# Moving the projections' shared elementwise work from GpSimd to the vector engine

## The chip, the cores and the metric

The kernel runs on one core of one Trainium2 chip. The metric is the device time of one execution in microseconds (us). The engines are named as the profile names them: PE is TensorE's matmul side and PEld its weight loads, DVE is the vector engine (VectorE), ACT is ScalarE, POOL is GpSimd, SP is SyncE, which only issues transfers here. Each engine carries out its own queue of instructions in order.

## The reference, cut to what matters

A trunk of two layers works on x of 1024 tokens by 1024 channels, float32:

```python
for l in range(2):
    h = rmsnorm(x, norm1_w[l])
    q, k, v, g, z, xbc, dt, gate, xin = split_proj(h @ w_in[l])
    y = concat([retention(q, k, v, g),            # 256 wide
                ssd(z, xbc, dt, ...),             # 512 wide
                rglru(gate, xin, ...)], -1)       # 256 wide
    x = x + y @ w_out[l]
    h = rmsnorm(x, norm2_w[l])
    u, v = split(causal_dwconv(h @ w_up[l]))      # 2 x 2816 wide, width-3 conv
    x = x + (gelu(u) * v) @ w_down[l]
return rmsnorm(x, final_norm_w)
```

The three mixers (retention, SSD, RG-LRU) are causal; what matters here is the four projections of each layer (into the mixers, out of them, up and down of the gated MLP).

## The kernel before, in words

**Layout.** Channels lie on the 128 partitions and tokens on the free axis, in two halves of 512 tokens. Almost every tile is 128 x 512 float32.

**Split operands.** A projection is computed at near float32 accuracy from operands split in two: ACT copies a tile to the matmul's type (the high part), and an elementwise subtraction `raw - high` gives the low part; three matmuls (high x high, high x low, low x high, the tuple `PASSES`) then stand for one. Weights arrive raw by DMA and are split on the chip in `part_split` (called by `part_of` and `wsplit`), activations in `split` and `load_split`. The subtraction of a weight's split has two forms. In the ordinary form it is one tensor-tensor instruction on DVE or on POOL. In the other, ACT first writes `-high` and POOL issues a DMA that adds the raw tile to it (`pool.dma_start(..., accum_op=ALU.add)`, "the accumulating transfer"). The flag `by_dma` allows the second form, and it is up only in the steady part of `products`.

**Who makes the low part.** `lo_engine` counts its calls and gives one call in `share` to DVE and the others to POOL; `share` is 3, and 2 inside `ffn_down`:

```python
    flip, share = [0], [3]

    def lo_engine():
        flip[0] += 1
        return dve if flip[0] % share[0] == 0 else pool
```

**Seven products for eight.** The up and in projections (`products`, class `Pair`) and the down projection (`ffn_down`) multiply 2 x 2 blocks in Strassen-Winograd form, so there are extra additions and subtractions of blocks, of weights (`Pair.prep`) and of activations (`blocks_b`); `sub(engine, ...)` (L714) carries out each one.

**Stages of a layer.**

- In projection: `blocks_a` or `blocks_raw` and `blocks_b` scale the activations by the norm, form the blocks t1, t2, t3, t4, b22 and split them, while the first pairs of outputs are already computed; then `products` goes through 12 pairs of output tiles with `by_dma` up.
- Mixers (`mixers`), with some work of POOL's own (L562, L563, L604, and L366, L370 in `lru`).
- Out projection (`out_proj`): 16 tiles of weights split by `wsplit`, mixer outputs loaded and split by `load_split` (L215, tiles `yl`), residual added (L699), and `squares` and `norm_sum` for the next norm. `squares` gives 6 of 8 squares to an accumulator on DVE and 2 to one on POOL; `norm_sum` adds both up on PE (tile `nst`).
- Up projection: `blocks_a`, `blocks_b` again, then `products` over 22 pairs, with convolution (L322) and gate (L939); results go to DRAM.
- Down projection (`ffn_down`): the *first loop*, 11 turns of 24 matmuls of 128 x 512 (tiles `dy`, `dx`, L1001) with four splits and three subtractions of activations each; then two more loops of 11 turns, and `last` (or `last` and `rest` in the second layer).

**What sets the order.** The kernel states each engine's instructions in program order, and a scheduler of the language then sets the order in each engine's queue before the program runs; it uses dependencies and its own estimates. The order on the chip is fixed.

## Time and profile before

| | |
|---|---|
| median of 3 runs | 2451.67 us (2446.18 to 2458.61) |
| the profiled execution, its own time | 2448.8 us |
| its span in the profile | 2447.0 us |
| PE matmuls busy | 2220.8 us, 91% of the span |
| DVE busy | 1967.6 us, 80% |
| ACT busy | 1278.5 us, 52% |
| POOL busy | 1096.3 us, 45% |
| mean granted TensorE clock | 0.963 of full speed |

The profile is one execution. Its page gives busy time and instruction counts by engine, the busiest groups of instructions, the waits and the transfers. A group is named by its source line, its engine, its operation and the tiles it writes and reads (`ws<-wr,ws`: the split weight tile `ws` from the raw tile `wr` and `ws` itself). An instruction's duration runs from its start to its end and includes the time in which it is held up after its start. PE's busy time is modelled and overlaps from one matmul to the next, so the pace of matmuls is read from their number in a stretch.

### The profile page before, as it was taken

The page shows a single profiled execution, that of the slowest core. Times are in us where ns is not written, and L with a number is a line of the kernel's source. Part 1 is how long each engine was busy: PE and PEld are TensorE (multiplying, and loading weights), DVE is VectorE, ACT ScalarE, POOL GpSimd, SP SyncE. Part 2 cuts the span into 40 slices and gives each one's busy share as a digit, 9 for nine tenths or more (in the row PEclk, how much of TensorE's full clock was granted, in tenths as well). Part 3 has the DMA queues.
Part 4 walks back from the last instruction along what each step waited for, and adds up shares of the span by engine and source line. Part 5 has one row for each costly group of instructions (what it writes and reads, how often), then busy time and mean ns, then how long its engine had stood idle before and what let it go on. Part 6 is the DMA issues. An engine that isn't in the chain of part 4 may idle for free. (4 is left out here: it accounts for less than half of the span.)

```text
span 2447.0 us, 32235 instructions
## 1 busy us (share of the span) xinstructions
PE 2220.8 (91%) x10646; PEld 1771.0 (72%) x10646; DVE 1967.6 (80%) x3242; ACT 1278.5 (52%) x2370; POOL 1096.3 (45%) x846
## 2 busy tenths in 40 slices
PE   5788978997999999989988988889989999998997
PEld 4566767775888888767765766777768888876776
DVE  7997768668888888887788876695797888889787
ACT  4356647454565666334444664664555665653343
POOL 4534433346434433554655332333473443437443
PEclk8999999998999999999989999999999999999999
DMA  4364685551666666843334647845426666575521
GB/s 175 103 149 115 162 255 192 163 188 44 141 158 150 146 147 159 273 156 123 104 112 125 152 108 203 260 135 184 145 71 163 148 159 157 139 231 182 168 70 70
DMA packets 176151, 371.98 MB, mean 152 GB/s; under 512 B 19440, under 2 KB 31856, under 8 KB 175984
## 3 DMA queue, kind: packets, MB, share of 16 engines
q1 hardware_dynamic: 135760, 297.55, 37.5%
q0 software_dynamic: 37440, 68.17, 16.6%
q10 hardware_dynamic: 2784, 4.20, 0.5%
q8 instruction: 84, 1.38, 0.2%
q14 instruction: 83, 0.68, 0.1%
HBM read 228.22 MB, written 69.27 MB: 122 GB/s over the span
## 5 line engine op out<-in xcount | busy, mean ns | idle before, releaser
L304 PE MATMUL up<-bh,ws 128*128 128x512 f32 x3840 | 1222.4, 399 | 59.8 <-ACT ws L235 33.4
L304 PEld LDWEIGHTS up<-bh,ws 128*128 128x128 f32 x3840 | 736.0, 192 | 229.9 <-ACT ws L235 35.2
L304 PE MATMUL up<-bl,ws 128*128 128x512 f32 x1920 | 763.8, 399 | 38.4 <-DVE bl L203 19.4
L235 ACT ACTIVATE ws<-wr 128x512 fp32r<-128x512 f32 x568 | 345.3, 621 | 304.9 <-issue 75.4
L304 PEld LDWEIGHTS up<-bl,ws 128*128 128x128 f32 x1920 | 368.2, 192 | 134.5 <-DVE bl L203 29.0
L242 POOL TENSOR_TENSOR ws<-wr,ws 128x512 fp32r<-128x512 f32 x164 | 241.8, 1483 | 268.1 <-ACT ws L235 252.2
L240 POOL DMA_DIRECT2D ws<-wr x222 | 198.4, 910 | 252.4 <-ACT ws L239 151.4
L714 POOL TENSOR_TENSOR wr<-wr 128x512 f32<-128x512 f32 x64 | 104.7, 1635 | 347.3 <-DVE wr L714 214.8
L1001 PE MATMUL dy<-ws,ws 128*128 128x512 f32 x792 | 214.0, 410 | 26.8 <-DVE ws L242 14.9
L1001 PEld LDWEIGHTS dy<-ws,ws 128*128 128x128 f32 x792 | 148.0, 194 | 83.7 <-DVE ws L242 35.0
L1001 PE MATMUL dx<-ws,ws 128*128 128x512 f32 x792 | 193.7, 393 | 4.1 <-DVE u L896 3.8
L1001 PEld LDWEIGHTS dx<-ws,ws 128*128 128x128 f32 x792 | 149.3, 189 | 37.7 <-DVE u L896 4.7
L322 DVE SCALAR_TENSOR_TENSOR fc<-c,smalls,fc 128x512 f32<-128x512 f32 (+2 forms) x176 | 175.1, 995 | 1.6 <-ACT fc L319 1.4
L242 DVE TENSOR_TENSOR ws<-wr,ws 128x512 fp32r<-128x512 f32 x182 | 142.0, 781 | 37.3 <-ACT ws L235 33.9
L322 DVE SCALAR_TENSOR_TENSOR fc<-u,smalls,fc 128x512 f32<-128x512 f32 (+2 forms) x176 | 140.4, 800 | 35.4 <-ACT fc L319 32.6
L304 PE MATMUL op<-yh,ws 128*128 128x512 f32 x512 | 165.2, 402 | 2.2 <-ACT yh L210 2.2
L239 ACT ACTIVATE ws<-ws 128x512 fp32r<-128x512 f32 x260 | 159.5, 625 | 4.6
L319 ACT ACTIVATE fc<-c,smalls 128x512 f32<-128x512 f32 x88 | 71.3, 810 | 131.2 <-DVE c L843 128.4
L242 DVE TENSOR_TENSOR ws<-g,ws 128x512 fp32r<-128x512 f32 (+1 forms) x94 | 113.0, 1229 | 29.9 <-ACT ws L235 29.7
L714 POOL TENSOR_TENSOR wr<-wr,s 128x512 f32<-128x512 f32 x64 | 103.4, 1615 | 58.3 <-DVE s L714 50.1
L714 DVE TENSOR_TENSOR wr<-wr,wr 128x512 f32<-128x512 f32 x64 | 45.1, 704 | 87.4 <-DMA wr<-in_w_up_dram 41.1
L304 PEld LDWEIGHTS op<-yh,ws 128*128 128x128 f32 x512 | 97.1, 192 | 23.0 <-ACT yh L210 3.3
(319 smaller groups left out, 3576.1 us busy)
## 6 DMA issues: line engine op xcount, KB each, us to landing
ws<-wr POOLq DMA_DIRECT2D x222, 256.0 KB, 4.2
wr<-in_w_up_dram SPq DMA_DIRECT2D x96, 512.0 KB, 4.4
wr<-in_w_dn_dram SPq DMA_DIRECT2D x66, 512.0 KB, 3.6
wr<-in_w_ct_dram SPq DMA_DIRECT2D x56, 512.0 KB, 4.3
wr<-in_w_o_dram SPq DMA_DIRECT2D x32, 512.0 KB, 4.7
g0scr<-fc SPq DMA_DIRECT2D x44, 256.0 KB, 3.6
g<-g0scr SPq DMA_DIRECT2D x44, 256.0 KB, 5.7
g1scr<-fc SPq DMA_DIRECT2D x44, 256.0 KB, 3.6
```

Source lines behind the costliest of these rows:

```text
L235: act.activation(w[:, 0, :m], raw, AF.Copy)
L239: act.activation(w[:, 1, :m], w[:, 0, :m].bitcast(F32), AF.Copy, scale=-1.0)
L240: pool.dma_start(w[:, 1, :m].bitcast(F32), raw, accum_op=ALU.add)
L242: eng.tensor_tensor(w[:, 1, :m], raw, w[:, 0, :m].bitcast(F32), op=ALU.subtract)
L304: pe.matmul(dst, W(k, a), A(k, b), start=first and i == 0, stop=last and i == n - 1)
L319: act.activation(dst, body(x), AF.Identity, bias=bias, scale=taps(n))
L322: dve.scalar_tensor_tensor(dst[:, o:HT], x[:, HALO - j + o : HALO - j + HT], taps(n - j), dst[:, o:HT], op0=ALU.mult, op1=ALU.add)
L714: eng.tensor_tensor(o, a, b, op=op)
L1001: pe.matmul(d[oc], w[:, a, P * oc : P * oc + P], t[:, b], start=not more and i == 0 and k == 0, stop=i == NP - 1 and k == 2, skip_group_ch ...
```

## The change

Elementwise work outside the mixers that POOL shared goes to DVE. `lo_engine` gives POOL only while `by_dma` is up, and whatever `part_split` gives to POOL is then the accumulating transfer. `squares` keeps one accumulator, on DVE. `blocks_b`, `Pair.scaled`, `Pair.prep` and `ffn_down` name DVE where they named POOL. POOL keeps the 260 accumulating transfers, its instructions in the mixers and a few of the final norm. The core of the diff:

```diff
-    flip, share = [0], [3]
+    flip = [0]
+
+    by_dma = [False]
     def lo_engine():
         flip[0] += 1
-        return dve if flip[0] % share[0] == 0 else pool
+        return pool if by_dma[0] and flip[0] % 3 else dve
...
     def part_split(w, raw, m, eng=None):
         act.activation(w[:, 0, :m], raw, AF.Copy)
         eng = eng or lo_engine()
-        if eng is pool and by_dma[0]:
+        if eng is pool:
...
-    def squares(X, spare=False, n=HT, f=t_tile):
-        acc = {}
-        for k in range(KD):
-            x = X(k)
-            eng = pool if k in (3, 6) else dve
...
+    def squares(X, n=HT, f=t_tile):
+        acc = f("nacc")[:, :n]
+        act.activation(acc, X(0), AF.Square)
+        for k in range(1, KD):
+            sq = f("nsq")[:, :n]
+            act.activation(sq, X(k), AF.Square)
+            dve.tensor_tensor(acc, acc, sq, op=ALU.add)
+        return [acc]
...
-            split(hi, lo, src, dve if name in ("t1", "b22") else engines[k % 2])
+            split(hi, lo, src, dve)
...
-                engines[i % 4 == 3].tensor_tensor(x, x, rows, op=ALU.mult)
+                dve.tensor_tensor(x, x, rows, op=ALU.mult)
...
-            sub(pool, XA[4 + k], XA[4 + k], t)
+            sub(dve, XA[4 + k], XA[4 + k], t)
...
-            sub(engines[k % 2], XB[k], XB[4 + k], XB[k])
+            sub(dve, XB[k], XB[4 + k], XB[k])
...
-                    pool.tensor_tensor(body(u), body(u), self.B["raw"], op=ALU.mult)
+                    dve.tensor_tensor(body(u), body(u), self.B["raw"], op=ALU.mult)
...
-            sub(pool, a21, a21, a22, ALU.add)
+            sub(dve, a21, a21, a22, ALU.add)
             w1 = part_of(a21)
-            sub(pool, a12, a12, s2)
+            sub(dve, a12, a12, s2)
...
-        share[0] = 2
...
-            sub(pool, b21, b21, T2[i])
+            sub(dve, b21, b21, T2[i])
...
-                part_split(t[:, :, e], G[i][1][:, e], hi - lo, pool)
+                part_split(t[:, :, e], G[i][1][:, e], hi - lo, dve)
...
-                    part_split(t[:, :, n * j : n * j + n], G[i + j][1][:, lo:], n, (dve, pool)[j % 2])
+                    part_split(t[:, :, n * j : n * j + n], G[i + j][1][:, lo:], n, dve)
```

In the built program POOL's queue shrinks from 851 instructions to 340 and DVE's grows from 3244 to 3765; Of the 511 that leave POOL 263 are splits `ws`, 128 the two sums of `Pair.prep`, 20 splits `yl`, 24 splits `bl` and 22 the subtractions `g<-g,t` of the down projection. ACT keeps 2354 and SP 935. On PE only the small matmuls of `norm_sum` change, from 160 instructions to 84.

**Place 1: one turn of the first loop of the down projection, first layer.** DVE's queue before (`g`, `t` are activation tiles, `ws` split tiles, `wr` raw weights):

```order
L242 TENSOR_TENSOR ws_9089<-g_9084,ws_9089 128x512
L242 TENSOR_TENSOR ws_9107<-g_9082,ws_9107 128x512
L714 TENSOR_TENSOR g_9082<-g_9122,g_9082 128x512
L714 TENSOR_TENSOR g_9122<-g_9124,g_9122 128x512
L714 TENSOR_TENSOR t_9128<-g_9124,g_9082 128x512
```

POOL's queue before, around the same turn:

```order
L242 TENSOR_TENSOR ws_9086<-wr_9080,ws_9086 128x512
L714 TENSOR_TENSOR g_9034<-g_9034,t_9078 128x512
L242 TENSOR_TENSOR ws_9104<-wr_9080,ws_9104 128x512
```

DVE's queue with the change:

```order
L243 TENSOR_TENSOR ws_9108<-wr_9102,ws_9108 128x512
L243 TENSOR_TENSOR ws_9111<-g_9106,ws_9111 128x512
L710 TENSOR_TENSOR g_9056<-g_9056,t_9100 128x512
L243 TENSOR_TENSOR ws_9126<-wr_9102,ws_9126 128x512
L243 TENSOR_TENSOR ws_9129<-g_9104,ws_9129 128x512
L710 TENSOR_TENSOR g_9104<-g_9144,g_9104 128x512
L710 TENSOR_TENSOR g_9144<-g_9146,g_9144 128x512
L710 TENSOR_TENSOR t_9150<-g_9146,g_9104 128x512
```

The two splits of weights and the subtraction `g<-g,t` now stand in DVE's queue, in front of the instructions that were there; a turn has 8 instructions on DVE and none on POOL.

**Place 2: the first norm of the program.** DVE's queue before, in the second half of the norm's small steps (`ny`, `nt`, 128 x 8) up to the diagonal tiles `ndg` that PE waits for (`lsp` is a constant worked out beside it):

```order
L191 SCALAR_TENSOR_TENSOR nt_456<-nt_456,nv_454 128x8
L1210 TENSOR_SCALAR lsp_730<-lsp_730 128x2
L192 SCALAR_TENSOR_TENSOR ny_455<-nt_456,ny_455 128x8
L190 TENSOR_TENSOR nt_456<-ny_455 128x8
L191 SCALAR_TENSOR_TENSOR nt_456<-nt_456,nv_454 128x8
L192 SCALAR_TENSOR_TENSOR ny_455<-nt_456,ny_455 128x8
```

DVE's queue with the change, in the same steps (`p`, `z` are constants worked out beside them):

```order
L710 TENSOR_TENSOR wr_822<-wr_822 128x512
L192 SCALAR_TENSOR_TENSOR ny_441<-nt_442,ny_441 128x8
L179 SCALAR_TENSOR_TENSOR p_719<-p_719,z_718 128x2
L243 TENSOR_TENSOR ws_827<-s_825,ws_827 128x512
L190 TENSOR_TENSOR nt_442<-ny_441 128x8
L179 SCALAR_TENSOR_TENSOR p_719<-p_719,z_718 128x2
L243 TENSOR_TENSOR ws_830<-wr_820,ws_830 128x512
L191 SCALAR_TENSOR_TENSOR nt_442<-nt_442,nv_440 128x8
L179 SCALAR_TENSOR_TENSOR p_719<-p_719,z_718 128x2
L243 TENSOR_TENSOR ws_834<-wr_822,ws_834 128x512
L192 SCALAR_TENSOR_TENSOR ny_441<-nt_442,ny_441 128x8
L710 TENSOR_TENSOR wr_820<-wr_820,s_825 128x512
```

Between the norm's small steps stand 128 x 512 instructions that POOL had: from `nv` to `ndg` DVE had two of them and now has eight.

## Rows read from the trace of the kernel before

**Rows 1.** The page, busy time, share of the span and instructions of each engine:
```profile
PE 2220.8 (91%) x10646; PEld 1771.0 (72%) x10646; DVE 1967.6 (80%) x3242; ACT 1278.5 (52%) x2370; POOL 1096.3 (45%) x846
```
**Rows 2.** Busy time by stage; after the stage: PE, PEld, DVE, ACT, POOL, clock, DMA:
```profile
8.00:122.00 114.00, 81.74 (x333) 56.89 (x334) 108.12 (x164) 46.12 (x86) 58.52 (x38) 0.87 0.39 130
350.00:457.00 107.00, 90.63 (x860) 77.80 (x861) 91.31 (x321) 71.54 (x213) 39.92 (x32) 0.95 0.58 187
457.00:542.00 85.00, 83.76 (x377) 67.40 (x378) 44.61 (x69) 38.32 (x65) 34.69 (x26) 0.96 0.60 192
542.00:620.00 78.00, 64.01 (x261) 46.78 (x261) 66.95 (x91) 38.16 (x61) 53.72 (x31) 0.89 0.19 62
620.00:991.00 371.00, 371.00 (x1638) 307.43 (x1637) 305.77 (x461) 216.66 (x357) 142.19 (x130) 1.00 0.67 159
991.00:1067.00 76.00, 64.06 (x264) 49.35 (x262) 71.41 (x66) 27.72 (x48) 50.97 (x31) 0.97 0.61 199
1067.00:1201.00 134.00, 128.99 (x526) 97.62 (x527) 106.12 (x127) 61.04 (x109) 65.13 (x45) 0.99 0.42 133
1234.00:1320.00 86.00, 65.61 (x278) 47.22 (x277) 79.93 (x108) 36.05 (x62) 54.22 (x30) 0.90 0.37 120
2186.00:2260.00 74.00, 62.84 (x264) 48.47 (x263) 71.44 (x66) 27.73 (x48) 50.99 (x31) 0.99 0.61 198
```
**Rows 3.** Timeline of DVE in the first down loop: start, us, engine, line, operation:
```profile
1025.31 1.77 DVE L242 TENSOR_TENSOR ws<-g,ws 128x512 fp32r<-128x512 f32 x1
1027.12 3.37 DVE L714 TENSOR_TENSOR g<-g,g 128x512 f32<-128x512 f32 x2
1030.41 0.68 DVE L714 TENSOR_TENSOR t<-g,g 128x512 f32<-128x512 f32 x1
1031.01 2.38 DVE L242 TENSOR_TENSOR ws<-g,ws 128x512 fp32r<-128x512 f32 x2
```
**Rows 4.** Timeline of POOL in the same stretch:
```profile
1026.50 3.44 POOL L242 TENSOR_TENSOR ws<-wr,ws 128x512 fp32r<-128x512 f32 x2
1031.16 1.67 POOL L714 TENSOR_TENSOR g<-g,t 128x512 f32<-128x512 f32 x1 [1.23 <-DVE t L714]
```
**Rows 5.** Timeline of DVE behind that loop, where POOL's last one has just ended:
```profile
1066.20 2.47 DVE L1006 TENSOR_TENSOR xd<-xd,dy 128x512 f32<-128x512 f32 x4
1068.60 2.47 DVE L1006 TENSOR_TENSOR xd<-xd,dx 128x512 f32<-128x512 f32 x4
```
**Rows 6.** Timeline of DVE in the first layer's lead-in:
```profile
50.82 5.24 DVE L756 SCALAR_TENSOR_TENSOR x<-x,first,nr 128x512 f32<-128x512 f32 x3 [1.41 <-ACT nr L1170]
61.80 0.74 DVE L752 SCALAR_TENSOR_TENSOR x<-x,first,rows 128x512 f32<-128x512 f32 x1
```
**Rows 7.** Groups of POOL in 542 to 620: count, busy, mean ns, idle before:
```profile
L714 POOL TENSOR_TENSOR xr<-xr,xr 128x512 f32<-128x512 f32 x2 | 10.7, 5393 | 2.6 <-DVE xr L714 2.6
```
**Rows 8.** Who waited for whom, whole span: us, times, longest:
```profile
PE up L304 <- DVE bl L203: 19.4, 14, 7.8
PE up L304 <- POOL bl L203: 18.6, 15, 2.2
PE dy L1001 <- DVE ws L242: 14.9, 23, 2.4
PE dy L1001 <- DVE xd L1006: 11.2, 4, 4.6
PE dx L1001 <- DVE u L896: 3.8, 2, 3.0
...
POOL ws L242 <- ACT ws L235: 323.0, 104, 10.4
POOL yl L215 <- ACT yh L210: 40.8, 16, 4.3
```
**Rows 9.** Groups of the whole span:
```profile
L242 DVE TENSOR_TENSOR ws<-wr,ws 128x512 fp32r<-128x512 f32 x182 | 142.0, 781 | 37.3 <-ACT ws L235 33.9
L268 PE MATMUL nst<-ones,nacc 128*64 128x1 f32 x320 | 12.2, 200 | 1.9 <-DVE nacc L1299 1.9
```

More of the change, by code (lines that the diff above doesn't have):

```diff
@@ L230, in wsplit @@
         return out_
-    by_dma = [False]
     def part_split(w, raw, m, eng=None):
@@ L245, in wk @@
         return lambda k, a: w[k // 4][:, a, P * (k % 4) : P * (k % 4) + P]
-    def squares(X, spare=False, n=HT, f=t_tile):
-        acc = {}
-        for k in range(KD):
-            x = X(k)
-            eng = pool if k in (3, 6) else dve
-            if eng not in acc:
-                acc[eng] = f("nacc")
-                act.activation(acc[eng][:, :n], x, AF.Square)
-                continue
-            sq = x if spare else f("nsq")[:, :n]
-            act.activation(sq, x, AF.Square)
-            eng.tensor_tensor(acc[eng][:, :n], acc[eng][:, :n], sq, op=ALU.add)
-        return list(acc.values())
+    def squares(X, n=HT, f=t_tile):
[6 more added lines that the diff above has]
+        return [acc]
     def norm_sum(*accs, n=HT):
@@ L740, in blocks_b @@
         act.activation(rows, pr, AF.Copy)
-        engines = (dve, pool)
         def put(name, k, src, fh, fl):
             hi, lo = fh("bh", dt=F32R), fl("bl", dt=F32R)
-            split(hi, lo, src, dve if name in ("t1", "b22") else engines[k % 2])
+            split(hi, lo, src, dve)
             B[name, k] = (hi, lo)
@@ L1234, in dt_c @@
             dts.extend(ssd_dt(l, h, dt[h]) for h in range(2))
-        share[0] = 3
         pairs = [in_pair(l, kind, i, B) for kind, i in ORDER]
@@ L1260, in hybrid_trunk @@
         spill(xs1, XB, 1)
-        share[0] = 3
         products([ffn_pair(l, j, B) for j in range(NF)], rest_of(B, XA, XB, sB, w2), {}, *((1, 2) if l else (1, 2)))
@@ L1298, in more @@
                 act.activation(sq, XB[k][:, e], AF.Square)
-                (dve if k >= 4 or not eng else pool).tensor_tensor(acc[eng], acc[eng], sq, op=ALU.add)
+                dve.tensor_tensor(acc[eng], acc[eng], sq, op=ALU.add)
             for k in range(4):
```

## The prediction

> **What bounds the kernel now.** I read the page's busy times first: PE is at 91% of the span, DVE at 80%, POOL at 45% [rows 1]. These are averages over stages with different limits, so the stage table comes next [rows 2]. In the up projection's steady part (620 to 991) PE is never idle and 1638 matmuls take 371 us, a pace of 0.227 us; DVE is busy for 306 us there, and what changes on DVE or POOL is hidden. The out projection (457 to 542) is the same, 83.8 us busy of 85. In the other stages shown PE has gaps and DVE is nearly full: 108 of 114 us in the first layer's lead-in (8 to 122), 67 of 78 in the up projection's lead-in, 71 of 76 in the first loop of the down projection, 80 of 86 in the second layer's lead-in. That is where the change can move the end. The list of waits agrees: PE waited 19.4 and 18.6 us for low parts `bl` from DVE and POOL, 14.9 for `ws`, 11.2 for the additions `xd`, 3.8 for `u`, 67.9 us together [rows 8].
>
> Then the timeline shows why DVE is full. With POOL at rest four 128 x 512 instructions take 2.47 us, and the next four start 2.40 us after the first: one costs 0.60 us of DVE's time when they follow each other, though each lasts 0.68 [rows 5]. In the first down loop the same instruction lasts about 1.7 us (one 1.77, two in 3.37) [rows 3] whenever a POOL instruction of 1.67 to 1.72 us runs [rows 4]; so do the lead-in's scalings, three in 5.24 us where one alone lasts 0.74 [rows 6]. The two engines do not work side by side here: a POOL instruction holds a DVE one up by about 1.77 - 0.68 = 1.09 us, and sometimes the reverse, as in the two POOL instructions that needed 5.39 us each [rows 7].
>
> **The change, part by part.** POOL's queue loses 851 - 340 = 511 instructions and DVE's gains 3765 - 3244 = 521. A moved one costs DVE 0.60 us and saves it between 0 (DVE was idle or not held up) and 1.09 us. So a move gains up to 0.49 and loses up to 0.60 us of DVE time, and what counts is which of the two holds where PE waits.
>
> *First loop of the down projection.* A turn repeats every 6.3 us before, from 1025.31 to the same instruction at 1031.01 + 0.60 = 1031.61 [rows 3]: two instructions at 0.60 and three held up to about 1.7, 6.3 us. DVE sets this pace, since PE needs 24 x 0.227 = 5.45 us for a turn. With the change a turn has 8 instructions, 8 x 0.60 = 4.8 us, under PE's 5.45: PE becomes the limit, and a turn gains 0.85 us. The loop took 76 us for 264 matmuls that need 264 x 0.227 = 60 us [rows 2]. Eleven turns would give 9.4; the first two still share DVE with the up projection's end, so I take 9 turns, 7.6 us, and 1.4 us more for the two waits at the loop's ends, for `u` at its start and the additions `xd` behind it (3.0 and 4.6 us longest [rows 8]), which come sooner when DVE is not behind. That makes 9 us a layer (bounds 0 and 14). The second layer's loop has the same numbers, 74 us with DVE at 71.4 [rows 2]: **18 us**.
>
> *First layer's lead-in, 8 to 122.* 37 of POOL's 38 instructions there move and add 37 x 0.60 = 22 us to DVE. If each had held DVE up, 40 us would go; with nothing held up, none. The rows shown are all held up, and DVE is at 95% [rows 2, 6], so I take about three quarters, 30 us: DVE's work falls by 8 us, and as DVE carries nearly the whole stage, so does the stage: **8 us** (bounds -6 and 15). The norm's small steps in it gain nothing: what held them up is replaced by instructions in their own queue.
>
> *Second layer's lead-in, 1234 to 1320.* The same blocks with DVE at 93%, some 28 instructions moved; PE waits less, so I take half: **4 us** (-4 and 8). *The up projection's two lead-ins*: POOL's long pair, 5.39 us each, goes [rows 7], but DVE is at 86% and as many instructions are added: 2 us each, **4 us** (-4 and 8).
>
> *The sums of squares.* One accumulator for two takes out (160 - 84)/160 of the `nst` matmuls, 12.2 us of PE's modelled busy time over the span [rows 9]: at most 5.8 us, of which I take **3 us**, since part lies in waits. The 10 additions more on DVE, 6 us in all, are inside the lead-ins' bounds.
>
> *At nothing.* The second and third down loops: 45 of POOL's instructions, but DVE is busy for 106 of 134 us and PE for 129 [rows 2], so a gain or loss of a few us is absorbed. The steady products and the out projection: PE covers them; uncovered, the 128 instructions of `Pair.prep` would cost 77 us of DVE time, against 65 us that DVE has idle in 620 to 991 alone, in one layer. The mixers: DVE has 91 of 107 us and few instructions move there; their POOL work stays and goes on holding DVE up. POOL's accumulating transfers lose the instructions that stood ahead of them; PE waits for little there. The scheduler has set a new order; its effect I cannot read from a row, and I take 0, with 10 us on either side.
>
> Sum: 18 + 8 + 4 + 4 + 3 = 37 us. Against the profiled execution, 2448.8 - 37 = 2411.8; the median of the runs is 2.9 us above that execution, which gives 2414.7. I put **2413 us** down.
>
> *A rule against the trace.* The rows above say that POOL's work costs DVE more than DVE's own would. The Trainium skill, "Perfetto Trace Analysis", section "Optimizing Scalar/DVE Operations", says that offloading even to GPSIMD may make sense when DVE is saturated, and warns that between these two it might not help because of a shared port. By the first half the change would be a loss, which is the third rival below; by the second it costs nothing. The same skill's "SBUF — State Buffer", section "Who interferes with whom", is stricter: a DVE instruction with two SBUF inputs and a GpSimd instruction that reads SBUF exclude each other. The trace agrees, 1.77 us for 0.68 [rows 3, 5].
>
> **The rivals.**
> 1. *Hidden anyway.* The gains of DVE are taken up by the next wait (ACT's high parts, loads), or the new order gives them back. For it: PE is at 91%, and the stages that gain are some 500 us of 2447. Against it: in the first down loop nothing else is close, ACT has 28 of 76 us. Time 2440 to 2460, no change.
> 2. *The waits move with the work* (slower). POOL stood idle for 323.0 us before splits, waiting for ACT, and 40.8 us before `yl` [rows 8]; idle POOL costs nothing, but DVE that waits holds back everything behind it. Its own splits of weights wait 37.3 us over 182 today, 0.20 each [rows 9]. At that price the 263 moved splits of `ws` bring 54 us of idle DVE and the 20 `yl` another 7, if DVE waits as now; it decides where DVE is the limit, above about 0.13 us a split (37/283). If all 61 us fell on the path, the time would be 2451.7 - 37 + 61 = 2476. Against it: most splits stand in stages with slack, and the scheduler puts them behind other work.
> 3. *DVE is not held up by POOL but by something that stays*, such as transfers or PE's reads. Then nothing is freed, and the moved work adds 0.60 each: 30 instructions, 18 us, in each first down loop, 22 in the first lead-in, 17 in each of three others, 109 us in all: 2561. The match of POOL's starts with DVE's long instructions speaks against it [rows 3, 4].
>
> That the change doesn't do what it says is out: the two queues' lengths show it.
>
> **How the numbers follow.** The terms' upper ends together give 28 + 15 + 8 + 8 + 6 = 65 us, their lower ends a loss of 14. Halfway to each end the gain is 51 and 12; with half of the order's 10 us above, the forecast's own range is 2451.7 - 56 = 2396 to 2439, and it has 0.75. Rival 1 has 0.14, rival 2 0.08, rival 3 0.03. About 0.5%, 12 us, is what a measurement of this kernel can tell from no change; 2439.4 is that bound. So faster 0.75, same 0.14, slower 0.11. The range is 2394 to 2448: it holds most of the forecast and half of rival 1.
>
> **What would show it.** In the profile after: 128 x 512 instructions of DVE at 0.68 us outside the mixers, none at 1.7; the first down loop at 62 to 68 us instead of 76, with turns of 5.5 us and PE without gaps; the first lead-in about 8 us shorter; DVE's busy time near its old 1968 us in spite of 521 more instructions; POOL under 350 us; the steady up projection unchanged at 371 us. Wrong would be: DVE idle before `ws` or `yl` for ACT for more than the 37 us of now while PE waits (rival 2), or DVE's long instructions still there (rival 3).

## The result, and the profile after

| | before | after |
|---|---|---|
| median of 4 runs each | 2450.77 us | 2345.66 us (2336.08 to 2347.68) |
| the profiled execution | 2448.8 us | 2346.2 us |
| its span | 2447.0 us | 2344.4 us |
| mean granted TensorE clock | 0.963 | 0.970 |

The kernel became faster by 105 us: the ratio is 0.9563, with a 95% interval of 0.9543 to 0.9583. The forecast was 2413 us with a range of 2394 to 2448, so the direction was right and the size was not: 105 us were gained where 38 were forecast.

The page's busy times after the change, to lay beside [rows 1]:

```profile
PE 2174.7 (93%) x10494; PEld 1758.3 (75%) x10494; DVE 1924.6 (82%) x3763; ACT 1288.4 (55%) x2370; POOL 302.6 (13%) x335
```

DVE carries 521 instructions more than before and is busy for 43 us less. At the 0.60 us that one costs when nothing stands in its way, the added ones are 521 x 0.60 = 313 us of work; so, as an estimate, 313 + 43 = 356 us of the old busy time was time in which DVE instructions were held up.

The stage table after. After each stretch: PE, PEld, DVE, ACT, POOL, granted clock, DMA share, GB/s. The rows are the mixers, the out projection, the up projection's lead-in and steady part, the first loop of the down projection, its second and third loops (all of layer one), the second layer's lead-in and the second layer's first down loop:

```profile
340.00:439.00 99.00, 88.11 (x882) 76.19 (x882) 87.50 (x337) 72.76 (x217) 26.01 (x22) 1.00 0.61 200
439.00:518.00 79.00, 78.74 (x360) 64.09 (x358) 55.26 (x99) 39.59 (x67) 0.00 (x0) 1.00 0.70 228
518.00:594.00 76.00, 61.44 (x240) 44.96 (x239) 66.46 (x124) 37.17 (x60) 0.00 (x0) 0.89 0.18 58
594.00:966.00 372.00, 372.00 (x1643) 308.03 (x1642) 298.45 (x498) 220.84 (x358) 75.94 (x88) 1.00 0.66 160
966.00:1026.00 60.00, 59.93 (x265) 49.26 (x264) 58.99 (x97) 26.31 (x45) 0.00 (x0) 1.00 0.71 238
1026.00:1149.00 123.00, 120.88 (x531) 99.05 (x530) 109.71 (x175) 63.51 (x112) 0.00 (x0) 1.00 0.49 152
1181.00:1260.00 79.00, 57.11 (x238) 43.12 (x237) 72.36 (x133) 36.09 (x61) 0.86 (x1) 0.83 0.39 124
2110.00:2172.00 62.00, 60.25 (x265) 49.20 (x264) 59.01 (x97) 26.33 (x45) 0.00 (x0) 1.00 0.73 240
```

Beside [rows 2], the first down loop fell from 76 to 60 us (74 to 62 in the second layer), the second and third loops from 134 to 123, the steady up projection did not move (371 and 372). In the down projection PE now runs at its pace: 265 x 0.227 = 60.2 and 531 x 0.227 = 120.5.

The timeline of DVE in the first down loop: start, duration, engine, line, operation, to lay beside [rows 3]:

```profile
1001.63 0.69 DVE L243 TENSOR_TENSOR ws<-wr,ws 128x512 fp32r<-128x512 f32 x1
1002.23 0.69 DVE L243 TENSOR_TENSOR ws<-g,ws 128x512 fp32r<-128x512 f32 x1
1002.84 0.69 DVE L710 TENSOR_TENSOR g<-g,t 128x512 f32<-128x512 f32 x1
1003.44 1.41 DVE L710 TENSOR_TENSOR g<-g,g 128x512 f32<-128x512 f32 x2
```

Each instruction lasts 0.69 us and the next starts 0.60 later; the 1.7 us ones are gone from this loop. PE's waits over the whole span (us, times, longest), beside [rows 8]:

```profile
PE up L300 <- ACT ws L236: 50.5, 8, 17.1
PE npr L279 <- DVE ndg L278: 15.2, 7, 5.0
PE up L300 <- DVE bl L206: 11.7, 17, 3.1
...
PE dy L995 <- DVE ws L243: 1.5, 3, 0.9
...
PE dx L995 <- DVE u L890: 0.8, 1, 0.8
```

The waits for `bl` fell from 38.0 us (DVE's and POOL's) to 11.7, those for `ws` in the down projection from 14.9 to 1.5, those for the additions `xd` from 11.2 to none.

**Where the 103 us of the two profiles went**, read at equal matmul counts, both layers together: in projections 17.1; mixers and out projections 30.2; up projections -0.1; first down loops with the wait behind them 28.1; second and third down loops 23.4; the rest of the down projections and the end 3.9. These places are from one profile of each kernel, and some of them vary by several us from profile to profile, as is shown below.

### The profile page after: what moved, and what is told of

The parts are those of the page before. It is cut to its first block, busy times and chain, and to the rows that moved or that the text cites. A ratio compares the mean times of both kernels' runs of the same rounds, so it can differ in the third digit from the quotient of the medians.

```text
span 2344.4 us, 31562 instructions
## 1 busy us (share of the span) xinstructions
PE 2174.7 (93%) x10494; PEld 1758.3 (75%) x10494; DVE 1924.6 (82%) x3763; ACT 1288.4 (55%) x2370; POOL 302.6 (13%) x335
## 3 DMA queue, kind: packets, MB, share of 16 engines
q0 software_dynamic: 37440, 68.17, 17.1%
## 4 chain that ended last, share of the span: by engine, by line
PE 65%; DVE 15%; DMA 8%; issue 7%; ACT 3%; SPq 1%; POOL 1%; DVEq 0%; POOLq 0%; ACTq 0%
PE up L300 43%; PE op L300 6%; PE dy L995 5%; PE dx L995 5%; PE dx L1071 2%; DMA ws<-wr 2%; DVE ws L243 2%; DVE bl L206 1%; DVE xb L318 1%; DMA cumb<-cumscr 1%; DMA tb<-in_rope_dram 1%; DMA g<-g1scr 1%; DMA g<-g0scr 1%; DVE g L710 1%; DMA wr<-in_w_ct_dram 1%
## 5 line engine op out<-in xcount | busy, mean ns | idle before, releaser
L300 PE MATMUL up<-bh,ws 128*128 128x512 f32 x3840 | 1228.2, 400 | 76.4 <-ACT ws L236 50.5
L300 PE MATMUL up<-bl,ws 128*128 128x512 f32 x1920 | 761.1, 398 | 11.8 <-DVE bl L206 11.7
L243 DVE TENSOR_TENSOR ws<-wr,ws 128x512 fp32r<-128x512 f32 x346 | 236.5, 688 | 61.0 <-ACT ws L236 54.9
L995 PE MATMUL dy<-ws,ws 128*128 128x512 f32 x792 | 192.2, 390 | 3.2 <-ACT ws L236 1.6
L318 DVE SCALAR_TENSOR_TENSOR fc<-u,smalls,fc 128x512 f32<-128x512 f32 (+2 forms) x176 | 131.0, 748 | 50.6 <-ACT fc L315 49.6
L300 PE MATMUL op<-yh,ws 128*128 128x512 f32 x512 | 160.5, 394 | 0.2 <-ACT yh L213 0.2
L318 DVE SCALAR_TENSOR_TENSOR fc<-c,smalls,fc 128x512 f32<-128x512 f32 (+2 forms) x176 | 131.2, 745 | 0.7 <-ACT fc L315 0.3
L243 DVE TENSOR_TENSOR ws<-g,ws 128x512 fp32r<-128x512 f32 (+1 forms) x165 | 103.1, 649 | 13.7 <-ACT ws L236 13.5
L236 ACT ACTIVATE ws<-g 128x512 fp32r<-128x512 f32 (+1 forms) x165 | 92.1, 590 | 39.7 <-PE dy L995 13.8
L300 PE MATMUL op<-yl,ws 128*128 128x512 f32 x256 | 100.3, 394 | 0.0
L236 ACT ACTIVATE ws<-s 128x512 fp32r<-128x512 f32 x64 | 40.4, 632 | 101.3 <-DVE s L710 92.4
```

Of the source, the lines that this page charges most:

```text
L236: act.activation(w[:, 0, :m], raw, AF.Copy)
L243: eng.tensor_tensor(w[:, 1, :m], raw, w[:, 0, :m].bitcast(F32), op=ALU.subtract)
L300: pe.matmul(dst, W(k, a), A(k, b), start=first and i == 0, stop=last and i == n - 1)
L318: dve.scalar_tensor_tensor(dst[:, o:HT], x[:, HALO - j + o : HALO - j + HT], taps(n - j), dst[:, o:HT], op0=ALU.mult, op1=ALU.add)
L995: pe.matmul(d[oc], w[:, a, P * oc : P * oc + P], t[:, b], start=not more and i == 0 and k == 0, stop=i == NP - 1 and k == 2, skip_group_ch ...
```

## The experiments

All of these kernels start from the changed kernel, unless the text says otherwise. Differences in time are those of medians against 2345.66 us; a kernel that starts from the kernel before is compared with that kernel's time beside it (2450.67 us for d_only, 2451.34 for o_only and p_only). Beside the various runs the kernel before took 2450.7 to 2454.0 us, so a difference of 3 us between two kernels measured at different times means little. A ratio is always to the kernel before, measured beside the run. POOL's moved instructions fall into four parts: 181 of the down projection, 64 splits of the out projection, 138 of the lead-ins (blocks, scalings, squares, first pairs' splits) and 128 sums of `Pair.prep`, 511 together.

### The down projection: back to POOL (u_down), and moved alone (d_only)

```diff
 u_down, against the changed kernel
+        share[0] = 2
...
-            sub(dve, b21, b21, T2[i])
+            sub(pool, b21, b21, T2[i])
...
-                part_split(t[:, :, e], G[i][1][:, e], hi - lo, dve)
+                part_split(t[:, :, e], G[i][1][:, e], hi - lo, pool)
...
 d_only, against the kernel before
-        share[0] = 2
+        share[0] = 1
...
-            sub(pool, b21, b21, T2[i])
+            sub(dve, b21, b21, T2[i])
...
```

> The changed kernel with the down projection alone put back: 181 instructions of ffn_down go to POOL again. Theory H (POOL's instructions hold DVE's up, and each stage gained by itself): the 28 and 24 us that the two down projections and about 3 that the tail gained come back, 2392 to 2402 us, first loop back to about 75 us, second and third to about 134. Rival O (the scheduler's new order made the gain, not the hold-up): less than half comes back, under 2372.

> The kernel before with the down projection alone moved to DVE (181 instructions). Theory H with stages that gain by themselves: the same 50 us as u_down showed from the other side, 2396 to 2406. If stages are not independent (a gain early is lost later): under 35 us.

Measured: u_down 2396.18 us, 50.5 more than the changed kernel, ratio to before 0.9774 (0.9756 to 0.9793). d_only 2401.99 us, 48.7 less than the kernel before, ratio 0.9801 (0.9786 to 0.9815). Both are inside their expected ranges, and nearly all of both lies inside the down projections and the end. At equal matmul counts the second and third loops took 134.6 us in the first layer and 133.7 in the second before, 122.9 and 122.0 with the change, 136.8 and 134.0 in u_down, 122.6 and 122.1 in d_only. DVE's timeline in the first down loop of u_down shows the held-up pairs again:

```profile
1000.05 2.38 DVE L245 TENSOR_TENSOR ws<-g,ws 128x512 fp32r<-128x512 f32 x2
1002.46 3.36 DVE L712 TENSOR_TENSOR g<-g,g 128x512 f32<-128x512 f32 x2
1005.75 0.68 DVE L712 TENSOR_TENSOR t<-g,g 128x512 f32<-128x512 f32 x1
```

What follows: the down projection's part of the change is worth about 50 us, half of the whole, and nearly the same whether the rest of the change is there (50.5) or not (48.7). It is the part for which the forecast had 18.

### Is it POOL's reading, or POOL's being busy? (g_read, g_write)

Both add useless POOL instructions to every second split of the three down loops; DVE then overwrites what they wrote. In g_read they read the raw tile, in g_write they only write. What the kernel computes stays the same.

```diff
 g_read
+        if ghost[0] and flip[0] % 2:
+            pool.tensor_tensor(w[:, 1, :m], raw, raw, op=ALU.subtract)
 g_write
+        if ghost[0] and flip[0] % 2:
+            pool.memset(w[:, 1, :m].bitcast(F32), 0.0)
+            pool.memset(w[:, 1, :m].bitcast(F32), 0.0)
```

> The changed kernel, and in the three down loops every second split has one POOL subtraction of the raw tile from itself, which DVE then overwrites: 132 useless POOL instructions that read SBUF, while DVE keeps all of its own work. Theory H (a POOL instruction holds a DVE one up by up to 1.09 us): a turn of 8 x 0.60 us gets 2 x 1.09 more, 7.0 against PE's 5.45, so 11 turns lose 17 us in each of the first two loops and somewhat less in the third: 40 to 45 us a layer, 2415 to 2435. Theory W (DVE loses only by waiting for POOL's result): no more than the next kernel loses. Rival 3 of the prediction (DVE is held up by something else): 2344 to 2350.

> As the kernel before, with two memsets of the same tile by POOL in the place of each subtraction: 264 POOL instructions that write the same places and are waited for in the same way, but read nothing. Theory H with the hold-up on POOL's reads alone: 2344 to 2354, DVE's instructions at 0.68 us. If POOL's writes hold DVE up as well: near the kernel before, over 2390. Theory W: the same loss in both.

Measured: g_read 2427.55 us, 82 more, ratio 0.9899 (0.9880 to 0.9917); g_write 2348.06 us, 2 more, ratio 0.9573 (0.9549 to 0.9598), an interval that overlaps the changed kernel's. Both are inside the ranges that theory H gave. Groups of g_read in 970 to 1180 us (count, busy, mean ns, idle before and for whom):

```profile
L245 DVE TENSOR_TENSOR ws<-wr,ws 128x512 fp32r<-128x512 f32 x39 | 38.4, 984 | 10.5 <-POOL ws L239 9.3
L245 DVE TENSOR_TENSOR ws<-a,ws 128x512 fp32r<-128x512 f32 x11 | 16.7, 1514 | 9.3 <-POOL ws L239 8.4 <-ACT ws L236 0.9
...
L239 POOL TENSOR_TENSOR ws<-wr 128x512 fp32r<-128x512 f32 x27 | 40.6, 1508 | 71.8 <-DVE wr L712 40.6 <-PE dy L997 21.8 <-PE dx L997 7.0
```

And of g_write in 970 to 1150:

```profile
L246 DVE TENSOR_TENSOR ws<-wr,ws 128x512 fp32r<-128x512 f32 x40 | 27.6, 690 | 6.3 <-ACT ws L236 5.0
...
L246 DVE TENSOR_TENSOR ws<-a,ws 128x512 fp32r<-128x512 f32 x11 | 7.6, 692 | 1.3 <-ACT ws L236 1.1
...
L239 POOL MEMSET ws<- 128x512 f32 x62 | 32.7, 528 | 105.9 <-PE dy L998 55.9 <-PE dx L998 50.0
```

What follows: 132 POOL instructions that read SBUF cost 82 us, 0.62 each; 264 that only write cost nothing that can be measured, though POOL is busy for about as long beside each split (2 x 0.53 us, against 1.1 to 1.5) and DVE must wait for it in the same places. DVE's splits last 984 and 1514 ns in the one and 690 in the other. So POOL's being busy makes no loss by itself; a POOL operation that reads does. The Trainium skill says the same in "SBUF — State Buffer", section "Who interferes with whom": a vector instruction with two SBUF inputs contends with a GpSimd instruction that reads SBUF, and not with one that only writes. What the pair does not separate is the reading from the kind of operation, a subtraction in the one and a memset in the other. The first two rows show a second cost that the forecast had not counted: DVE also stood idle for 9.3 + 8.4 us until POOL's instruction ended, since that is late as well.

### The out projection's splits: back to POOL (u_out), and moved alone (o_only)

```diff
 u_out, against the changed kernel
         after = mixers(l, dts, skip(l))
+        share[0] = 3
...
 o_only, against the kernel before
         after = mixers(l, dts, skip(l))
+        share[0] = 1
```

> The changed kernel with two of three splits of the out projection (weights and mixer outputs, 64 instructions) on POOL again. Theory H: the stretch from the last matmul of the in projection to the end of the out projection gained 17 us in the first layer and 13 in the second; nearly all comes back, 2368 to 2376 us, and the small steps of the gated norm in the mixers (128 x 2) last longer again. Rival O: under 2356. Rival Q (POOL's own mixer work was late behind those splits in POOL's queue): as H in time, but the small DVE steps stay at 0.18 us and PE waits for POOL's xd instead.

> The kernel before with the out projections' splits alone on DVE; all else as before. Additive theory (each moved piece is worth what its undoing cost): about 14 us faster than before, 2433 to 2441, of which some 4 us in each layer's mixers (111 to 115 us before, between the last matmul of the in projection and the 64th of the out projection) because the 11 splits that POOL carried out there no longer hold DVE up, and some 3 us in the rest of each out projection (79 to 80 us before). Rival A: the mixers' whole gain of 8 to 12 us a layer belongs to these splits, and the undoing showed only part of it: mixers at 103 to 104 us, time 2424 to 2431. Rival B: the mixers gained through the order and the granted clock alone: mixers as before within 2 us, time 2443 to 2447.

Measured: u_out 2360.12 us, 14.5 more, ratio 0.9620 (0.9602 to 0.9639). o_only 2434.52 us, 16.8 less than before, ratio 0.9933 (0.9911 to 0.9954). u_out is a miss: its time lies between the two ranges that were expected. By place it gave back 16 of the 30 us of the mixers and out projections. Its rival Q did not come: PE's wait for POOL's `xd` is 2.5 us there and 2.3 in the changed kernel, and the small steps (`gtt`, 128 x 2) last 214 ns, against 182 in the changed kernel and 338 before. o_only came out in its expected range, but with more of the gain in the mixers than was expected of them. The first layer's mixers (last matmul of the in projection to the 64th of the out projection), then the rest of the out projection; columns as in the stage table. Before:

```profile
347.00:462.00 115.00, 98.41 (x903) 84.38 (x902) 96.01 (x332) 75.88 (x222) 41.22 (x33) 0.96 0.59 192
462.00:542.00 80.00, 78.76 (x354) 63.17 (x353) 41.81 (x64) 36.10 (x61) 33.39 (x25) 0.96 0.60 192
```

After:

```profile
341.00:444.00 103.00, 92.11 (x901) 79.57 (x900) 90.72 (x340) 74.56 (x220) 26.01 (x22) 1.00 0.62 201
444.00:518.00 74.00, 73.74 (x336) 59.92 (x335) 51.04 (x91) 37.46 (x63) 0.00 (x0) 1.00 0.69 227
```

o_only:

```profile
353.00:459.00 106.00, 94.45 (x900) 81.17 (x899) 92.83 (x339) 74.22 (x218) 27.54 (x22) 0.98 0.60 191
459.00:535.00 76.00, 75.92 (x358) 61.73 (x357) 46.58 (x84) 37.77 (x64) 8.68 (x7) 1.00 0.68 226
```

With the splits alone moved, the mixers go from 115 to 106 us and the out projection from 80 to 76; in the second layer from 111 to 105 and from 79 to 75. That is 23 of the 30 us that the whole change brings there. POOL's column says why: 33 instructions before, 22 after. The 11 that left are splits for the out projection (6 `ws`, 5 `yl`) which the scheduler had put ahead into the mixers' time. The first layer's in projection ended 5 us later in o_only, which the edit does not touch.

The mixers also vary without any edit to them. In u_down, g_write and sq2 (below) PE, DVE and POOL have the changed kernel's order there within a handful of instructions, and the mixers took 102 to 107 us, with the granted clock between 0.97 and 1.00. So 3 to 4 us of a place in one profile mean nothing, and the last 3 us between 106 and 103 stay unassigned. The first in projection varies as much: with one and the same order but for a few instructions it ended at 348.4 us in the kernel before, 353.5 in d_only and 353.8 in o_only, and at 342.0 in the changed kernel, 338.4 in u_down, 340.0 in g_read and 339.4 in g_write. The two groups do not overlap, but the 6 us that the profiles of before and after give to this place could as well be 12.

### The lead-ins and the weights' sums (u_lead, u_prep, p_only)

u_lead gives blocks, scalings, squares and the first pairs' splits back to POOL as they were, and with the squares the second accumulator and its small matmuls on PE; u_prep the two sums of `Pair.prep`; p_only moves these two sums alone, from the kernel before.

```diff
 u_lead, against the changed kernel
-            split(hi, lo, src, dve)
+            split(hi, lo, src, dve if name in ("t1", "b22") else engines[k % 2])
...
-            sub(dve, XA[4 + k], XA[4 + k], t)
+            sub(pool, XA[4 + k], XA[4 + k], t)
...
 u_prep, against the changed kernel (p_only is the reverse)
-            sub(dve, a21, a21, a22, ALU.add)
+            sub(pool, a21, a21, a22, ALU.add)
...
-            sub(dve, a12, a12, s2)
+            sub(pool, a12, a12, s2)
```

> The changed kernel with the lead-ins put back: blocks_b, squares, Pair.scaled and the splits of the first pairs (138 instructions) on POOL again. Theory H: the lead-ins gained 6 and 4 us and the up projections' none, so 8 to 16 us come back, 2354 to 2362. Rival O: 0 to 5, 2346 to 2351.

> The changed kernel with the two sums of Pair.prep (128 instructions) on POOL again. Theory H: DVE is held up, but PE covers it in the steady products: 0 to 4 us, 2346 to 2350, with the steady up projection unchanged and any difference in the in projections. Rival O: the same; a loss of over 8 us would show that PE does not cover DVE there.

> The kernel before with the two sums of Pair.prep alone on DVE (128 instructions); all else as before. Additive theory: what the undoing cost, 25 us, comes back, 2423 to 2430, mainly in the in projections' leading pairs and behind them, nothing in the up projection's steady part. Rival, the pieces overlap (the four undoings together cost 120 us where the change brought 105): as long as POOL keeps its other work there DVE goes on being held up, 10 us or less is gained, 2440 to 2450.

Measured: u_lead 2375.41 us, 29.8 more, ratio 0.9685 (0.9666 to 0.9705); u_prep 2371.15 us, 25.5 more, ratio 0.9677 (0.9649 to 0.9704). Both are misses: u_lead lost about twice the upper end of what was expected, u_prep six times. p_only 2441.59 us, 9.8 less than before, ratio 0.9960 (0.9945 to 0.9974): its rival came out, the pieces overlap. The four undoings cost 50.5 + 14.5 + 29.8 + 25.5 = 120 us, the change as a whole brought 105. u_prep lost 10 us in the first layer's in projection, 6 in the second's, 5 in the first mixers and none in the steady up projection. In u_prep DVE's queue is shorter by 128 x 0.60 = 77 us of work, and no stage gained by it. p_only does not show the reverse of this by place: its in projections took 353.3 and 312.7 us, against 348.4 and 315.1 before (and 353.5 and 316.7 in d_only), while its mixers and out projections are 8 us shorter together. Of u_lead's loss 16 us lie in the in projections and 8 in the first mixers, where only the scheduler's order is another; the up projections' lead-ins became 2 to 3 us shorter.

### Reading or being busy, once more, in Pair.prep (g_prep, g_prepw)

```diff
 g_prep
+            for _ in range(2):
+                pool.tensor_tensor(s2, mat..., mat..., op=ALU.add)
 g_prepw
+            for _ in range(4):
+                pool.memset(s2, 0.0)
```

> The changed kernel, and in Pair.prep two useless POOL additions of constants into the tile s2 before DVE overwrites it: 128 POOL instructions that read SBUF, in the place and number of those that u_prep put back, but early, so that DVE seldom waits for their results, and with DVE keeping all of its work. u_prep lost 25 us. Theory H (the loss is DVE held up): 20 to 35 us lost, 2366 to 2381, since DVE keeps the moved work as well. Theory L (the loss in u_prep is POOL's long result, 1.3 to 1.7 us for 0.7, on the way to the split weights): 0 to 8 us, 2345 to 2354.

> As g_prep with four memsets (about 0.53 us each) for the two additions, so POOL is busy as long, writes the same tile and is waited for in the same way, but reads nothing. Theory H: 0 to 5 us, 2343 to 2351. If it loses as much as g_prep, POOL's occupation (accumulating transfers late in its queue) or the wait for s2 is the cause, not the hold-up.

Measured: g_prep 2391.67 us, 46 more, ratio 0.9750 (0.9731 to 0.9770); g_prepw 2353.71 us, 8 more, ratio 0.9602 (0.9586 to 0.9618). The 128 reading instructions cost 0.36 us each, the 256 writing ones almost nothing: 6.5 of their 8 us lie in the second layer's mixers, where the edit put nothing but the scheduler had set another order (109 us there, clock 0.97). The direction is as in the down projection; g_prep lost 10 us more than the upper end of its range, g_prepw 3. In g_prep POOL reads constants and not the weights that DVE works on, so the two engines need not read the same data for the loss.

### One accumulator or two (sq2)

```diff
-        return [acc]
...
+            eng = int(k in (3, 6))
...
+            dve.tensor_tensor(acc[eng][:, :n], acc[eng][:, :n], sq, op=ALU.add)
+        return list(acc.values())
```

> The changed kernel with two accumulators in squares again, both on DVE: 76 more small matmuls of PE in six sums and 12 fewer additions of DVE; POOL is as in the changed kernel. The prediction's term for the small matmuls: 3 us slower, 2347 to 2350. Rival O (the order that the scheduler finds, which any such edit moves, is worth several us): a difference of over 4 us either way, and stretches that the edit doesn't touch, as the mixers, change by several us.

Measured: 2349.51 us, 3.9 more, ratio 0.9577 (0.9548 to 0.9607). The interval overlaps the changed kernel's; the 3 us that the forecast gave to the sums of squares are neither shown nor refuted.

### What POOL kept, moved too (m_dve)

```diff
-        pool.tensor_tensor(h8(xd), h8(xs), b8(dt), op=ALU.mult)
-        pool.tensor_tensor(h8(dxd), h8(xs), b8(dec), op=ALU.mult)
+        dve.tensor_tensor(h8(xd), h8(xs), b8(dt), op=ALU.mult)
+        dve.tensor_tensor(h8(dxd), h8(xs), b8(dec), op=ALU.mult)
```

and three more such lines, 60 instructions of the mixers.

> The changed kernel with POOL's part of the mixers on DVE too (60 instructions: xd, dxd, ss in the SSD chunks, two in each RG-LRU tile). Theory H: DVE is 85 of 95 us busy in the mixers; it gets 22 x 0.60 = 13 us more in a layer and is freed of hold-ups such as 986 ns for 683 of the products by cbt (5 us) and those of small steps; the chain through xd becomes 1.1 us shorter at each of 8 chunks. Between -6 and +6 us: 2338 to 2352, faster if what ends last is the chain, slower if it is DVE's work.

Measured: 2370.0 us, 24 more, ratio 0.9661 (0.9636 to 0.9686), a miss. The first layer's mixers took 112 us instead of 103, the second's 115. Here is a piece of them, columns as in the stage table:

```profile
410.00:414.00 4.00, 3.67 (x38) 3.01 (x37) 3.01 (x16) 2.57 (x8) 0.00 (x0) 1.00 0.90 318
414.00:418.00 4.00, 1.22 (x9) 0.85 (x8) 4.00 (x14) 4.00 (x12) 0.00 (x0) 1.00 0.03 12
418.00:422.00 4.00, 2.80 (x13) 2.37 (x13) 3.44 (x16) 0.98 (x3) 0.00 (x0) 0.56 0.25 72
422.00:426.00 4.00, 4.00 (x42) 3.60 (x42) 2.36 (x6) 0.91 (x4) 0.00 (x0) 0.58 0.54 163
```

DVE and ACT are full from 414 to 418, PE works for 1.22 of 4 us, and in the next 8 us the granted clock is 0.56 and 0.58, near the lower of its two levels (1.2 GHz). At that level a 128 x 128 matmul of these mixers starts 213 ns after the one before it, at the full clock 112. Such falls make the stage's mean clock 0.92, against 1.00 in the changed kernel, and PE's modelled time there 99.3 us instead of 92.1. So of the 9 us that the first mixers lose some 7 are slower matmuls, behind gaps of PE. Whether DVE's fuller queue left these gaps or the new order, which differs on PE too, is not separated. What POOL kept it should keep.

### More of the accumulating transfers (c_dma)

A version meant to beat both kernels: `by_dma` is up from the first pair on, so that 57 more splits leave DVE as transfers.

```diff
+        by_dma[0] = True
...
-            by_dma[0] = j >= n
```

> A version that may beat both: the changed kernel with by_dma up from the first pair of products on, so that two of three of the first pairs' splits (57 instructions) go from DVE to the accumulating transfer. By H, DVE sheds some 34 us of work over the four lead-ins, where it is busy for 94% of the time, and POOL's DMA issue holds nothing up: 5 to 20 us faster, 2326 to 2341. Against it, rival D: a split through the transfer lands some 4 us later, and PE, which already waits for ACT's and the transfers' parts there, waits longer: 2346 to 2365.

Measured: 2369.5 us, 24 more, ratio 0.9666 (0.9652 to 0.9680), slower even than its rival D expected. PE's waits in it:

```profile
PE up L300 <- ACT ws L236: 54.8, 11, 17.1
PE npr L279 <- DVE ndg L278: 31.2, 8, 10.5
PE up L300 <- DVE bl L206: 18.7, 30, 3.0
```

The waits for the norm's `ndg` and for `bl` grew by 16 and 7 us, though DVE has fewer instructions, and most of the loss lies in the lead-ins, 13 us of it in those of the up projections. Each such split gives ACT a second pass and needs a transfer, where a 0.69 us subtraction was enough; which of the two delays the lead-ins was not taken apart. No kernel tried here is faster than the changed one.

## Why the prediction was wrong in size

**Right.** What the two engines do to each other, and its sign. DVE's 128 x 512 instructions last 0.69 us: of its tensor-tensor and scalar-tensor-tensor instructions of this size outside the mixers 285 of 1886 lasted over 1 us before, and 7 of 2366 do after; POOL is busy for 303 us; the first down loops take 60 and 62 us; the steady up projection is unchanged; DVE's busy time, forecast near 1968 us, is 1925. Rival 1 (hidden anyway) is refuted by the time itself, rival 3 (something else holds DVE up) by u_down and by g_read beside g_write. Rival 2 (DVE idle for ACT's high parts) did not come. By the letter of its sign DVE's idle time before `ws<-wr,ws` did grow, from 37.3 to 61.0 us, but over 346 splits instead of 182, 0.18 each for 0.20 [rows 9]; before all splits `ws` together DVE waited 74.3 us for ACT before and 70.0 after, and PE's idle time over the span fell from 216 to 161 us.

**The step that failed: "At nothing".** The places that the forecast put at nothing gave 23 + 30 = 53 us, most of the 67 us that it missed. "The second and third down loops: ... DVE is busy for 106 of 134 us and PE for 129, so a gain or loss of a few us is absorbed." They gave 23.4 us, 11.7 in each layer. Two errors stand in that sentence.

First, PE's 129 us is the modelled busy time, which overlaps and also fills short gaps. The text's own pace, 528 x 0.227 = 120 us, left 14 us of gaps in each layer; of these 2 to 3 remain.

Second, DVE's slack of 28 us was taken for cover. These are the groups of the kernel before in 1067 to 1201 us (DVE, then POOL):

```profile
L242 DVE TENSOR_TENSOR ws<-g,ws 128x512 fp32r<-128x512 f32 x22 | 31.0, 1440 | 8.6 <-ACT ws L235 8.6
L242 DVE TENSOR_TENSOR ws<-t,ws 128x512 fp32r<-128x512 f32 x11 | 14.5, 1321 | 4.6 <-ACT ws L235 4.6
...
L714 DVE TENSOR_TENSOR g<-a,wr 128x512 f32<-128x512 f32 x10 | 6.9, 692 | 10.7 <-POOL ws L242 10.7
...
L242 POOL TENSOR_TENSOR ws<-g,ws 128x512 fp32r<-128x512 f32 x23 | 38.3, 1668 | 0.3 <-ACT ws L235 0.3
L242 POOL TENSOR_TENSOR ws<-a,ws 128x512 fp32r<-128x512 f32 x11 | 14.4, 1308 | 34.3 <-ACT ws L235 34.3
```

And the changed kernel in 1027 to 1149:

```profile
L243 DVE TENSOR_TENSOR ws<-g,ws 128x512 fp32r<-128x512 f32 x46 | 29.6, 685 | 3.1 <-ACT ws L236 3.1
...
L243 DVE TENSOR_TENSOR ws<-t,ws 128x512 fp32r<-128x512 f32 x11 | 7.5, 684 | 0.0
```

A low part that took 1.3 to 1.7 us on either engine takes 0.69, and DVE no longer waits 1.07 us in ten turns for POOL's late split. DVE's busy time in these loops even rose, from 106 to 109 us, and the loops became 12 us shorter. The same lateness stands in the waits of PE's weight loads, which need the split tiles; before in 1072 to 1201 us, then after in 1027 to 1149:

```profile
PEld dy L1001 <- DVE ws L242: 10.9, 18, 1.6
```

```profile
PEld dy L995 <- DVE ws L243: 0.7, 1, 0.7
```

The sum went by DVE's total work, where what PE waited for was the lateness of single instructions in a chain. A low engine share does not cover that. u_down and d_only show that these loops' gain comes from their own moved instructions, and g_write, in which POOL is busy there without reading, has them at 123.3 and 122.3 us, g_read at 150.6 and 149.7.

**The same sentence for the out projection and the mixers** ("few instructions move there") failed by 30 us. The count of 32 POOL instructions in [rows 2] was read as the mixers' own work; a third of them were the out projection's splits, put ahead by the scheduler, and o_only gives 23 us to them, u_out 16. Of the out projection it was said that PE covers it, 83.8 us busy of 85, modelled time again and at a granted clock of 0.96 [rows 2]. The mixers have long chains of small steps, and these were held up as well: in 350 to 460 us before, `gtt` steps of 128 x 2 averaged 338 ns, in the changed kernel's 350 to 450 182 ns:

```profile
L191 DVE SCALAR_TENSOR_TENSOR gtt<-gtt,gv 128x2 f32<-128x2 f32 x24 | 8.1, 338 | 0.2
```

```profile
L191 DVE SCALAR_TENSOR_TENSOR gtt<-gtt,gv 128x2 f32<-128x2 f32 x24 | 4.4, 182 | 0.1
```

What such steps are worth in the mixers' time was not measured by itself.

**The first down loop, 9 us a layer,** gave 16.1 and 12.0. PE runs at its pace of 60 us, so a turn is what was forecast; the terms for its two ends were too small. For the waits at both ends 1.4 us were taken, and the wait behind the loop alone gave 4.7 in each layer; the first half of the loop, where DVE's work from the up projection's end still lies, gave 7.1 and 3.0. Not all of that first half belongs to the down projection's own instructions: d_only has 3.7 and 2.9 of it, p_only 2.7 and 0.4. The upper bound of 14 was nearer.

**The lead-ins, 8 + 4 + 4 us.** By place the in projections gained 17.1 us for 12 forecast, and the up projection's lead-ins nothing for 4. In both places together PE's largest wait is for ACT's `ws`, 33.4 us before and 50.5 after: some of what DVE no longer delays waits for ACT instead. In the up projections that wait was absent before and is 10.8 us after, where 7.4 us for POOL's `bl` went. The long pair of POOL that the up projection's terms rested on was misread, too [rows 7]: 5.39 us is the mean of two very different ones (duration in ns: least, median, most).

```profile
L714 POOL TENSOR_TENSOR xr<-xr,xr x2: 1287/5393/9499, 579.0 to 588.4; 128x512 f32<-128x512 f32 x2
```

During the one that took 9.5 us DVE started 14 instructions of 128 x 512 with two inputs, 0.60 us after each other and 0.68 us long. So the hold-up goes either way: here POOL was held up and DVE not at all, and to move that instruction freed no time of DVE. The term "at nothing" for `Pair.prep` holds in the steady up projection, 0 us, but not elsewhere: undone with the rest moved (u_prep) it cost 25 us, 16 of them in the in projections, and moved alone (p_only) it brought 10, which its profile has elsewhere.

**The sums of squares, 3 us,** stay open: sq2 measured 3.9 us, inside the noise.

**The order of the scheduler, 0 with 10 on either side,** was fair: single places moved by 3 to 7 us for it or for the granted clock, and the pieces' overlap is 120 - 105 = 15 us. Which of the two makes these shifts where the order differs is not separated by any run.

By instruction, undoing cost 0.28 us in the down projection, 0.23 in the out projection, 0.22 in the lead-ins, 0.20 in `Pair.prep`. These lie within the forecast's bounds for DVE's time, a loss of 0.60 to a gain of 0.49; the error was to grant the gain only where DVE was nearly full, and too little of it there.

## What to carry to other kernels

Before elementwise work is shared between DVE and POOL, look in the timeline at how long DVE's two-input instructions last while POOL reads SBUF; where 0.69 us becomes 1.7, sharing takes more than it gives, even where DVE's total share looks low. Whether PE covers a stage is read from its matmul count times the pace of a full stage, not from its modelled busy time, and which POOL instructions stand in a stage from the names in the trace, not from the program. POOL remains good for what only writes, memsets here, and for what it kept in the mixers, which cost 24 us when DVE took it over.

## What the runs showed of the hardware that was not expected

That 264 POOL memsets beside DVE's splits cost 2 us, and 132 reading instructions in their place 82. That one POOL instruction of 128 x 512 lasted 9.5 us while DVE carried out 14 two-input ones at their usual 0.68. That the mixers, with the same order on PE, DVE and POOL but for a handful of instructions, took 102 to 107 us from one kernel's profile to another's, with the mean granted clock at 1.00 to 0.97; and that a stretch in which PE worked for 1.22 of 4 us was followed by 8 us at a clock of 0.56 to 0.58, in part of which a 128 x 128 matmul took 213 ns instead of 112, so that a gap cost more than its own length.
